# Where the first expert's weights may land: a new memory layout, earlier first loads, and 4 MB gate-and-up loads in a two-block transformer kernel

## The chip, the cores and the metric

One core of a Trainium2 chip runs the whole program. The metric is device time in microseconds (us); three runs before the change gave 1537.29, 1537.30 and 1537.64 us, median 1537.3.

## The reference, cut to what matters

Two transformer blocks on 256 tokens of width 1024, all in float32. The change touches the end of the second block: cross attention to 256 memory rows (4 heads of 128), then a mixture of 16 experts in which every expert takes its 32 best tokens, then a last norm.

```python
x = first_block(...)                                   # mixer + SwiGLU
x = x + concat(pool, mlstm, attention) @ w_out         # second block
# cross attention; mem @ ca_wkv gives k, v; 4 heads of 128
q = rmsnorm(x, norm_mem_g) @ ca_wq                     # 1024 -> 512
x = x + (softmax(q k^T * 128**-0.5) v) @ ca_wo         # 512 -> 1024
# experts
h = rmsnorm(x, norm_ffn_g)
aff = softmax(h @ router_w)                            # 256 x 16
gates, idx = top_k(aff.T, 32)                          # 32 tokens per expert
for e in range(16):
    ga, up = split(h[idx[e]] @ w_gu[e])                # w_gu[e]: 1024 x 4096, 16.8 MB
    y[e] = (silu(ga) * up) @ w_down[e]                 # w_down[e]: 2048 x 1024, 8.4 MB
x = x + scatter_add(y * gates)
return rmsnorm(x, final_norm_g)
```

The experts' weights are 402.7 MB, each byte used once.

## The kernel before, in words

All loads are issued by SyncE (SP), which takes its instructions in order: a load that waits holds up every load behind it. A layer under the kernel (tile pools) records which memory each tile occupies and makes an instruction wait for the last reader or writer of whatever lay there before. The order of instructions on each engine comes from that layer's planner, which mixes independent work; a load that names `queued(e_last)` keeps its place behind the one before it. Loads share eight completion semaphores in rotation, so each also waits until the load eight before it has landed.

`cross` (line 988) loads `ca_wq` in two 1 MB units and splits each into a high and a low part for three-pass products; then for each half t of the tokens come q, the scores against `mK`, a softmax, the values with `mV` into the tile `o`, and the product of `o` with `ca_wo` (line 1035), whose result goes to x. `route` (1040) transposes x and computes the router's logits.

`moe` (1061) loads the first expert's weights before the routing is known: `eload` issues 2 MB loads (128 partitions of 16 KB) into 12 slots. Eight slots are pools `e0` to `e7` on the right side of the memory, four are buffers of the pool `big`, which held the split weights. An expert needs eight gate-and-up loads (block k holds input features 128k to 128k+127, line 1151) and four down loads, so the first expert fills the 12 slots once, and the 13th load waits until TensorE has read the first slot. The products read each slot with eight matmuls (line 1154), or eight for a down load (1187).

The top-k chain (1093 to 1120) and the gather `xs` (1136) come before the first expert product. The last expert's down weights come in column pieces (line 1234: seven loads of 1 MB, then 0.5, 0.25 and 0.25 MB), so that the last piece leaves little work behind it.

`xt` is the pool of the normalised, transposed input (tiles `xh`, `xl`); `mkv` holds `mK` and `mV`; `rawp` holds the loads before they are split; `ca` holds `o`.

## Time and profile before

| | |
|---|---|
| median of three runs | 1537.3 us |
| profiled execution: time, span of its core | 1536.87 us, 1535.2 us |
| TensorE busy, share of the span | 1190.9 us, 78% |
| VectorE, ScalarE busy | 434.3 us, 28%; 351.7 us, 23% |
| DMA queue of SP: bytes, share of 16 engines' span | 501.86 MB, 82.0% |
| chain that ended last, share by engine | DMA 54%, PE 2%, SP's queue 2% |

The span is the time from the first to the last instruction; 1.7 us lie around it. The chain of waits is followed back from the last instruction to whatever released each step. In a timeline a row gives start, length and instructions merged (x). "SPq" is SP's queue; a load is "landed" when its semaphore has been raised.

### The profile page before, as it was taken

Reading aid. Unit: us, or ns where it says so; the run is one execution under the profiler, and the core shown is the slowest. Engines: PE = TensorE matmul, PEld = TensorE weight load, DVE = VectorE, ACT = ScalarE, POOL = GpSimd, SP = SyncE. Lnnn points to the kernel's source line nnn. Section 1 sums busy time; section 2 is a strip of 40 time slices with the busy share of each in tenths; the row PEclk is TensorE's granted clock in tenths of the full one; section 3 lists DMA queues with packets and bytes.
Section 4 is the critical chain, followed back from the end, with each engine's and each line's share of the span. In section 5 each row is a group of like instructions: output and inputs, shape, how many; then the busy total and the mean of one; then the engine's idle time right before and its main releaser. Section 6 shows DMA issues by size and latency. Waiting matters only on the chain.

```text
span 1535.2 us, 17874 instructions
## 1 busy us (share of the span) xinstructions
PE 1190.9 (78%) x7685; PEld 677.8 (44%) x7685; DVE 434.3 (28%) x851; ACT 351.7 (23%) x608; POOL 5.0 (0%) x16
## 2 busy tenths in 40 slices
PE   7999998999999999696765656666656666566665
PEld 5988988999978776221121111112111112111112
DVE  6744667544577764300000000000000000000002
ACT  6554545443456733000000000000000000000002
POOL 1000000000000000000000000000000000000000
PEclk9999999999999999797888878879788689888798
DMA  9754547555533369899999999999999999999996
GB/s 301 222 165 140 163 138 230 190 182 188 182 108 115 111 234 429 370 427 428 426 428 429 425 428 427 427 427 426 428 428 426 428 426 428 427 427 427 427 424 243
DMA packets 109103, 503.00 MB, mean 328 GB/s; under 512 B 10059, under 2 KB 64095, under 8 KB 84960
## 3 DMA queue, kind: packets, MB, share of 16 engines
q1 hardware_dynamic: 109024, 501.86, 82.0%
q8 instruction: 60, 0.98, 0.3%
q14 instruction: 19, 0.16, 0.0%
HBM read 500.79 MB, written 1.05 MB: 327 GB/s over the span
## 4 chain that ended last, share of the span: by engine, by line
DMA 54%; PE 2%; SPq 2%; DVE 1%; issue 0%; ACT 0%; DVEq 0%
DMA eraw<-in_expert_w_gu_dram 36%; DMA eraw<-in_expert_w_down_dram 18%; SPq L1234 2%; PE sm L1154 1%; PE sm L1187 1%; PE sm L1136 0%; DVE tk L1109 0%; DVE m L1108 0%; PE acc L1201 0%; DVE OH L1120 0%; DVE x L1243 0%; ACT L1174 0%; PE sm L1178 0%; DVE es L1175 0%; DVE eraw L1251 0%
## 5 line engine op out<-in xcount | busy, mean ns | idle before, releaser
L1154 PE MATMUL sm<-eraw,xs 128*32 128x512 f32 x2048 | 324.3, 742 | 190.2 <-DMA eraw<-in_expert_w_gu_dram 190.2
L1154 PEld LDWEIGHTS sm<-eraw,xs 128*32 128x32 f32 x2048 | 62.5, 123 | 425.6 <-DMA eraw<-in_expert_w_gu_dram 290.7
L1187 PE MATMUL sm<-eraw,aT 128*32 128x512 f32 (+2 forms) x1088 | 170.3, 762 | 86.8 <-DMA eraw<-in_expert_w_down_dram 79.4
L68 DVE TENSOR_TENSOR whl<-raw,whl 128x1024 fp32r<-128x1024 f32 x166 | 198.8, 1221 | 116.9 <-ACT whl L67 116.7
L67 ACT ACTIVATE whl<-raw 128x1024 fp32r<-128x1024 f32 x166 | 168.3, 1052 | 86.0 <-issue 56.1
L1175 DVE SCALAR_TENSOR_TENSOR es<-sm,rsl,es 128x512 f32<-128x512 f32 x16 | 12.0, 751 | 463.0 <-PE sm L1154 460.0
L1187 PEld LDWEIGHTS sm<-eraw,aT 128*32 128x32 f32 x1088 | 34.7, 128 | 202.9 <-DMA eraw<-in_expert_w_down_dram 125.0
L1174 ACT ACTIVATE es<-sm,rsl 128x512 f32<-128x512 f32 x16 | 11.0, 687 | 426.1 <-PE sm L1154 426.1
L86 PE MATMUL acc<-xh,whl 128*128 128x256 f32 x704 | 94.2, 283 | 0.0
L86 PE MATMUL sm<-xh,whl 128*128 128x256 f32 x704 | 92.3, 284 | 0.8 <-ACT xh L118 0.8
L86 PEld LDWEIGHTS sm<-xh,whl 128*128 128x128 f32 x704 | 88.7, 192 | 1.8 <-ACT xh L118 1.2
L86 PEld LDWEIGHTS acc<-xh,whl 128*128 128x128 f32 x704 | 87.4, 188 | 0.8
L1199 DVE COPY ys<-sm 128x512 f32<-128x512 f32 (+2 forms) x18 | 11.4, 632 | 242.1 <-PE acc L1201 237.6
L86 PE MATMUL acc<-whl,xh 128*128 128x512 f32 x256 | 70.5, 407 | 0.7 <-DVE rstd L127 0.5
L1201 PE MATMUL acc<-ys,ogT 128*128 128x512 f32 (+2 forms) x136 | 67.0, 617 | 5.1 <-DVE ys L1199 4.3
L1197 ACT ACTIVATE ys<-sm 128x512 f32<-128x512 f32 x16 | 9.6, 597 | 232.9 <-PE sm L1187 232.9
L86 PE MATMUL acc<-whl,aH 128*128 128x512 f32 x176 | 55.9, 390 | 0.0
L86 PEld LDWEIGHTS acc<-whl,xh 128*128 128x128 f32 x256 | 47.3, 190 | 13.7 <-ACT xh L118 1.4
L86 PE MATMUL acc<-xl,whl 128*128 128x256 f32 x352 | 50.9, 283 | 0.0
L86 PE MATMUL sm<-xl,whl 128*128 128x256 f32 x352 | 49.0, 281 | 0.0
L1201 PEld LDWEIGHTS acc<-ys,ogT 128*128 128x128 f32 x136 | 24.2, 202 | 54.1 <-issue 20.5
L86 PEld LDWEIGHTS acc<-xl,whl 128*128 128x128 f32 x352 | 45.3, 189 | 0.4
(361 smaller groups left out, 1099.8 us busy)
## 6 DMA issues: line engine op xcount, KB each, us to landing
eraw<-in_expert_w_gu_dram SPq DMA_DIRECT2D x128, 2048.0 KB, 39.1
eraw<-in_expert_w_down_dram SPq DMA_DIRECT2D x60, 2048.0 KB, 39.1
raw<-in_w_in_dram SPq DMA_DIRECT2D x34, 1024.0 KB, 5.5
raw<-in_w_gate_dram SPq DMA_DIRECT2D x11, 1024.0 KB, 5.3
raw<-in_w_up_dram SPq DMA_DIRECT2D x11, 1024.0 KB, 5.5
raw<-in_w_down_dram SPq DMA_DIRECT2D x11, 1024.0 KB, 4.9
raw<-in_w_out_dram SPq DMA_DIRECT2D x8, 1024.0 KB, 5.7
eraw<-in_expert_w_down_dram SPq DMA_DIRECT2D x7, 1024.0 KB, 27.8
```

Source lines behind the costliest of these rows:

```text
L67: nc.scalar.activation(H[:, k], raw[:, k], AF.Copy)
L68: self.at["L"] = nc.vector.tensor_tensor(L[:, k], raw[:, k], H[:, k].bitcast(F32), OP.subtract).ins
L86: nc.tensor.matmul(out, l[i], r[j], start=first and p == 0 and q == 0, stop=last and p == 2 and q == n - 1)
L1154: nc.tensor.matmul(dst[32 * j:32 * j + 32, :], xs[:, k, 32 * q:32 * q + 32], raw[:, o + 512 * j:o + 512 * j + 512], start=k == 0, stop=k = ...
L1174: nc.scalar.activation(s, G, AF.Silu, scale=rs)
L1175: nc.vector.scalar_tensor_tensor(s, U, rs, s, OP.mult, OP.mult)
L1187: nc.tensor.matmul(y[c0][32 * c:32 * c + 32, 0:n], aT[:, c, 32 * j:32 * j + 32], raw[:, o:o + n], start=j == 0, stop=j == 3, tile_position ...
L1197: nc.scalar.activation(ys, y[c0][:, 0:n], AF.Copy)
L1199: nc.vector.tensor_copy(ys, y[c0][:, 0:n])
L1201: nc.tensor.matmul(out[t], ogT[:, t * 128:(t + 1) * 128], ys, start=first, stop=last)
L1234: nc.sync.dma_start(raws[j].rearrange("p (i n) -> p i n", i=4)[:, :, c0:c0 + m], rows(j)[:, :, c0:c0 + m])
```

## The change

1. Feature order. Block k of the expert input is no longer features 128k to 128k+127 but every second feature of a group of 256 (`feats`). The transposes of x in `route` and in the gather, the router's weights and the gain `gT` follow this order, so that the rows of two blocks lie side by side in memory: a partition's part of blocks k and k+1 is 32 KB in one piece.
2. Memory. `mkv` moves to the left side, under `big`, and takes `o`; the pairs of high and low parts become one tile of 16 KB (`xhl`, `memHL`).
3. First expert. Four slots (`r0` to `r3`) are opened in `cross`. Its first four loads are chained in SP's order with `ca_wo`: two behind `ca_wq`, then the first half of `ca_wo`, two more, then the second half. The next eight take slots `l0` to `l3`, `xt` and `l4` to `l6`; `l0` to `l6` are opened when `rawp`, `big` and `mkv` are closed. The product with `ca_wo` runs column half by column half.
4. From the third expert on. The slots are opened anew as six of 32 KB. Gate-and-up weights come in four 4 MB loads per expert; down weights still in 2 MB loads, two to a slot.
5. The last expert. The first two of four down blocks come whole (2 MB each); the other two in column pieces as before.

SP's queue at the end of cross attention. `raw` are the loads of `ca_wq` and `ca_wo`, `eraw` the expert loads, `gain` the gain before cross attention; behind "waits" stand the semaphores (DMAHW: landed loads; PE, DVE, Activation: work done by that engine). Before:

```order
L50 DMA raw<-in_ca_wq_dram 128x4x512 [waits DMAHW6_49,DVE_49,Activation_49]
L50 DMA raw<-in_ca_wq_dram 128x4x512 [waits DMAHW7_49,DVE_49,Activation_49]
L50 DMA raw<-in_ca_wo_dram 128x4x512 [waits DMAHW0_49,DVE_49]
L50 DMA raw<-in_ca_wo_dram 128x4x512 [waits DMAHW1_49,DVE_49]
L1084 DMA eraw<-in_expert_w_gu_dram 128x4096 [waits PE_49,Pool_49]
L1084 DMA eraw<-in_expert_w_gu_dram 128x4096 [waits PE_49]
L1084 DMA eraw<-in_expert_w_gu_dram 128x4096 x3
L1084 DMA eraw<-in_expert_w_gu_dram 128x4096 [waits DMAHW2_49,DVE_49,PE_49]
L1084 DMA eraw<-in_expert_w_gu_dram 128x4096 [waits DMAHW3_49]
L1084 DMA eraw<-in_expert_w_gu_dram 128x4096 [waits DMAHW4_49]
L1084 DMA eraw<-in_expert_w_down_dram 128x4096 [waits DMAHW5_49,PE_49]
```

Now:

```order
L56 DMA raw<-in_ca_wq_dram 128x4x512 [waits DMAHW5_49,DVE_49,Activation_49]
L149 DMA gain<-in_norm_mem_g_dram 128x1024
L56 DMA raw<-in_ca_wq_dram 128x4x512 [waits DMAHW6_49,DVE_49,Activation_49]
L1069 DMA eraw<-in_expert_w_gu_dram 128x4096 [waits PE_49,Pool_49]
L1069 DMA eraw<-in_expert_w_gu_dram 128x4096 [waits DVE_49,PE_49]
L56 DMA raw<-in_ca_wo_dram 128x4x512 [waits DMAHW7_49,DVE_49]
L1069 DMA eraw<-in_expert_w_gu_dram 128x4096 [waits PE_49]
L1069 DMA eraw<-in_expert_w_gu_dram 128x4096
L56 DMA raw<-in_ca_wo_dram 128x4x512 [waits DMAHW0_49,DVE_49]
L1069 DMA eraw<-in_expert_w_gu_dram 128x4096 [waits DMAHW1_49,PE_49,Activation_49]
L1069 DMA eraw<-in_expert_w_gu_dram 128x4096 [waits DMAHW2_49]
L1069 DMA eraw<-in_expert_w_gu_dram 128x4096 [waits DMAHW3_49,DVE_49]
```

Four expert loads moved ahead of the last `ca_wo` load, and the fifth now waits for TensorE and ScalarE. Its slot, `l0`, lies from byte 31552 to 47936 of each partition; `o` lies from 28480 to 32576, so the two share the last 1024 bytes of `o`. The semaphore value that the load waits for is reached by the last matmul of `o` with `ca_wo` for the second half of the tokens (L1056); ScalarE's is the write of `o`.

TensorE at the same place: `mV` the values, `raw,o` the product with `ca_wo`, `ident,x` the transposes of x, `rw,xf` the router's logits. Before:

```order
L1023 MATMUL po<-apT,mV 128x128 x4
L1035 MATMUL acc<-raw,o 128x512 x3
L982 MATMUL sm<-ident,aE 128x128 x4
L1048 MATMUL at<-ident,x 128x128 x8
L1023 MATMUL po<-apT,mV 128x128 x4
L1059 MATMUL at<-rw,xf 128x16 x4
L1035 MATMUL acc<-raw,o 128x512
L1059 MATMUL at<-rw,xf 128x16 x4
L1035 MATMUL acc<-raw,o 128x512 x7
L1048 MATMUL at<-ident,x 128x128 x8
```

Now:

```order
L1045 MATMUL po<-apT,mV 128x128 x4
L1090 MATMUL at<-ident,x 128x128 x4
L991 MATMUL sm<-ident,aE 128x128 x4
L1045 MATMUL po<-apT,mV 128x128 x4
L1056 MATMUL acc<-raw,o 128x512 x5
L1090 MATMUL at<-ident,x 128x128 x4
L1101 MATMUL at<-rw,xf 128x16 x4
L1056 MATMUL acc<-raw,o 128x512
L1101 MATMUL at<-rw,xf 128x16 x4
L1056 MATMUL acc<-raw,o 128x512 x6
L1090 MATMUL at<-ident,x 128x128 x8
```

Behind the last matmuls on the values (`mV`) there were 8 of the 16 products with `ca_wo`; now there are 12, with four more transposes among them.

The diff (left out: the renamed arguments of `mem_T`, which now uses `pair_T`, and the closing of a pool at the end):

```diff
@@ -18,6 +18,12 @@
 EPS = 1e-6
 NEG = -1e30
 D = 1024
+def feats(k):
+    o = 256 * (k // 2) + k % 2
+    return slice(o, o + 255, 2)
 def bcast(ap1d, parts=128):
@@ -154,12 +160,16 @@
             return ss[:, 2:3]
         return ss[:, 0:1]
+    def pair_T(self, pool, name, **kw):
+        HL = self.sb(pool, [128, 2, 8, 256], name, F32R, **kw)
+        return HL[:, 0], HL[:, 1]
     def norm_T(self, x, gname):
         nc = self.nc
         g = self.gain(gname)
-        H = self.sb(self.xt, [128, 8, 256], "xh", F32R, tag="xh")
-        L = self.sb(self.xt, [128, 8, 256], "xl", F32R, tag="xl")
+        H, L = self.pair_T(self.xt, "xhl", tag="e")
         def factor(t):
             h = self.work.tile([128, D], F32, name="hn", tag="work")
@@ -221,7 +231,9 @@
         self.xt = self.open("xt", 1, self.xtp, "right")
         self.NR, self.NH = 3, 4
         self.ep = self.open("ep", 1)
-        self.big = self.open("big", 1)
+        bigst = ExitStack()
+        self.mkv = self.open("mkv", 1, bigst)
+        self.big = self.open("big", 1, bigst)
         rawst = ExitStack()
         self.rawp = self.open("rawp", 1, rawst)
         st = ExitStack()
@@ -235,8 +247,6 @@
         nc.sync.dma_start(x[:, 1, :], xr[:, 1, :])
         first = [self.unit(a["w_in"][0], u, 1024) for u in range(2)]
         self.constants()
-        mkv = ExitStack()
-        self.mkv = self.open("mkv", 1, mkv, "right")
         memp = ExitStack()
         self.memp = self.open("memp", 1, memp, "right")
         for t in range(2):
@@ -245,7 +255,7 @@
         xT = self.block1_ffn(xT, wg)
         xT = self.block2_mix(*xT, memp, st)
         self.cross(xT)
-        self.close(rawst, mkv, self.xtp)
+        self.close(rawst, bigst)
         self.moe()
         self.psum_st.close()
...
@@ -504,10 +514,9 @@
         nc.tensor.matmul(po[:, 128:256], va[:, 1, h * 128:(h + 1) * 128], pT[:, 256:384], start=False, stop=True)
         nc.scalar.activation(qT[:, h, :], po[:, 0:256], AF.Copy)
-    def mem_T(self, pool, tags=(None, None), psum="sm"):
+    def mem_T(self, pool, psum="sm"):
         nc, tc = self.nc, self.tc
-        H = self.sb(pool, [128, 8, 256], "memH", F32R, tag=tags[0])
-        L = self.sb(pool, [128, 8, 256], "memL", F32R, tag=tags[1])
+        H, L = self.pair_T(pool, "memHL", tag="e")
         m = self.rawp.tile([128, 2, D], F32, name="mem", tag="raw", bufs=self.NR)
         nc.sync.dma_start(m, self.a["mem_2"][0].rearrange("(t p) d -> p t d", p=128))
         for t in range(2):
...
@@ -990,16 +999,29 @@
         NE = 16
         with ExitStack() as es:
             ca, cw = self.open("ca", 1, es), self.open("caw", 2, es)
-            o = self.sb(ca, [128, 4, 256], "o")
+            o = self.sb(self.mkv, [128, 4, 256], "o")
+            self.early = ExitStack()
+            self.ewt = [self.open("r%d" % i, 1, self.early, "right") for i in range(4)]
+            self.e_last, self.loaded = [], []
             rt = self.ep
             rw = self.sb(rt, [128, 8, NE], "rw")
-            nc.sync.dma_start(rw, a["router_w_2"][0].rearrange("(k p) e -> p k e", p=128))
+            nc.sync.dma_start(rw.rearrange("p (k i) e -> p k i e", i=2),
+                              a["router_w_2"][0].rearrange("(k p i) e -> p k i e", p=128, i=2))
             gT = self.gT = self.sb(rt, [128, 8], "gT")
-            nc.sync.dma_start(gT, a["norm_ffn_g_2"][0].rearrange("(k p) -> p k", p=128))
+            nc.sync.dma_start(gT.rearrange("p (k i) -> p k i", i=2),
+                              a["norm_ffn_g_2"][0].rearrange("(k p i) -> p k i", p=128, i=2))
             nc.vector.tensor_tensor(rw, rw, gT[:, :, None].to_broadcast([128, 8, NE]), OP.mult)
             self.rw = rw
             w = self.cols(a["ca_wq_2"][0], 0)
+            for k in range(2):
+                self.loaded.append(self.gu_block(self.ewt[k], k))
+            wo = [self.chained(lambda: self.unit(a["ca_wo_2"][0], 0, 0))]
+            for k in range(2, 4):
+                self.loaded.append(self.gu_block(self.ewt[k], k))
+            wo.append(self.chained(lambda: self.unit(a["ca_wo_2"][0], 0, 512)))
             for t in range(2):
                 c = slice(t * 128, (t + 1) * 128)
                 acc = self.gemm_t(xT, w, t)
@@ -1027,14 +1049,35 @@
             self.r4, self.r4_ins, self.logits = [None] * 2, [None] * 2, [None] * 2
             self.rc = self.sb(rt, [128, 2], "rc")
-            w = [self.unit(a["ca_wo_2"][0], 0, 512 * c) for c in range(2)]
             for t in range(2):
                 acc = [self.ps("acc") for _ in range(2)]
-                for k in range(4):
-                    for c in range(2):
-                        nc.tensor.matmul(acc[c], o[:, k, t * 128:(t + 1) * 128], w[c][:, k, :], start=k == 0, stop=k == 3)
+                for c in range(2):
+                    for k in range(4):
+                        nc.tensor.matmul(acc[c], o[:, k, t * 128:(t + 1) * 128], wo[c][:, k, :], start=k == 0, stop=k == 3)
                 self.add_x(t, acc)
                 self.route(t, cw)
+    def chained(self, f):
+        n = len(self.nc.cur_bb.bb.instructions)
+        with self.queued(self.e_last):
+            r = f()
+        return r
+    def eload(self, dst, src):
+        with self.queued(self.e_last):
+            self.e_last[:] = [self.nc.sync.dma_start(dst, src).ins]
+    def gu_block(self, pool, k, e=0):
+        raw = pool.tile([128, 4096], F32, name="eraw", tag="e")
+        self.eload(raw, self.gu_rows(e, k)[:, k % 2])
+        return raw
+    def gu_rows(self, e, k):
+        o = 256 * (k // 2)
+        return self.a["expert_w_gu_2"][0][e, o:o + 256, :].rearrange("(p i) n -> p i n", i=2)
     def route(self, t, cw):
@@ -1044,8 +1087,7 @@
         for q in range(2):
             p = self.ps("at")
             for k in range(4):
-                c = 4 * q + k
-                nc.tensor.transpose(p[:, k * 128:(k + 1) * 128], x[:, t, c * 128:(c + 1) * 128], self.ident)
+                nc.tensor.transpose(p[:, k * 128:(k + 1) * 128], x[:, t, feats(4 * q + k)], self.ident)
             p = p.rearrange("p (k c) -> p k c", k=4)
             if q == 0:
                 nc.vector.tensor_copy(xf[:, 0:4], p)
@@ -1061,29 +1103,25 @@
     def moe(self):
         tc, nc, a = self.tc, self.nc, self.a
         NE, CAP = 16, 32
-        wgu, wdn = a["expert_w_gu_2"][0], a["expert_w_down_2"][0]
+        wdn = a["expert_w_down_2"][0]
         with ExitStack() as es:
             ep, x = self.ep, self.x
             ew = self.open("ew", 1, es)
             OH = self.sb(ep, [128, 2, NE, CAP], "OH")
             aff = self.sb(ep, [128, 2, NE], "aff")
-            e_ = [(self.open("e%d" % i, 1, es, "right"), "e", 1) for i in range(8)]
-            hl = (self.big, "hl", self.NH)
-            slots = e_[2:5] + [hl] * 2 + e_[:1] + [hl] * 2 + e_[1:2] + e_[5:8]
-            n_unit, e_last = [0], []
+            slot_st = ExitStack()
+            left = [self.open("l%d" % i, 1, slot_st) for i in range(7)]
+            pools = self.ewt + left[0:4] + [self.xt] + left[4:7]
+            n_slot = [4]
             def slot():
-                pool, tag, bufs = slots[n_unit[0] % len(slots)]
-                n_unit[0] += 1
-                return pool.tile([128, 4096], F32, name="eraw", tag=tag, bufs=bufs)
-            def eload(src):
-                raw = slot()
-                with self.queued(e_last):
-                    e_last[:] = [nc.sync.dma_start(raw, src).ins]
-                return raw
+                pool = pools[n_slot[0] % len(pools)]
+                n_slot[0] += 1
+                return pool.tile([128, 4096 if len(pools) == 12 else 8192], F32, name="eraw", tag="e")
+            eload = self.eload
             io = self.sb(ep, [128, CAP], "io")
             nc.gpsimd.iota(io, pattern=[[1, CAP]], base=1, channel_multiplier=0, allow_small_or_imprecise_dtypes=True)
             st = self.small.tile([128, 16], F32, name="rs", tag="st8", bufs=4)
@@ -1133,7 +1171,7 @@
                             if i == 0:
                                 pg[kk] = self.ps()
                             for t in range(2):
-                                nc.tensor.matmul(pg[kk][:, i * 128:(i + 1) * 128], x[:, t, k * 128:(k + 1) * 128],
+                                nc.tensor.matmul(pg[kk][:, i * 128:(i + 1) * 128], x[:, t, feats(k)],
                                                  OH[:, t, e:e + 4, :].rearrange("p e s -> p (e s)"), start=t == 0, stop=t == 1)
                         kk, i = divmod(k0, 4)
                         nc.vector.tensor_tensor(xs[:, k0:k0 + n, :],
@@ -1147,8 +1185,22 @@
                         gather(0, 1)
                         gather(1, 1)
                 G, U = self.ps(), self.ps()
+                if e == 2:
+                    self.close(slot_st, self.early, self.xtp)
+                    left = [self.open("ll%d" % i, 1, slot_st) for i in range(6)]
+                    pools, n_slot[0] = [left[i] for i in (4, 5, 0, 1, 2, 3)], 0
                 for k in range(8):
-                    raw = eload(wgu[e, 128 * k:128 * k + 128, :])
+                    src = self.gu_rows(e, k)
+                    if e == 0 and k < 4:
+                        raw = self.loaded[k]
+                    elif e < 2:
+                        raw = slot()
+                        eload(raw, src[:, k % 2])
+                    else:
+                        if k % 2 == 0:
+                            both = slot()
+                            eload(both, src.rearrange("p i n -> p (i n)"))
+                        raw = both[:, 4096 * (k % 2):4096 * (k % 2) + 4096]
                     for o, dst in ((0, G), (2048, U)):
                         for j in range(4):
                             nc.tensor.matmul(dst[32 * j:32 * j + 32, :], xs[:, k, 32 * q:32 * q + 32],
@@ -1202,7 +1254,13 @@
                 if e < NE - 1:
                     for j in range(4):
-                        raw = eload(rows(j).rearrange("p i n -> p (i n)"))
+                        if e < 2:
+                            raw = slot()
+                        else:
+                            if j % 2 == 0:
+                                both = slot()
+                            raw = both[:, 4096 * (j % 2):4096 * (j % 2) + 4096]
+                        eload(raw, rows(j).rearrange("p i n -> p (i n)"))
                         for n in range(2):
                             down(j, raw, 512 * n, 512)
                     for n in range(2):
@@ -1219,7 +1277,7 @@
                 p = self.ps()
                 nc.tensor.matmul(p, self.ones[0:1, :], grow[:, 512 * n:512 * n + 512], start=True, stop=True)
                 nc.scalar.activation(g[:, 512 * n:512 * n + 512], p, AF.Copy)
-            fo = slot()[:, 0:2 * D].rearrange("p (t n) -> p t n", t=2)
+            fo = end[:, 4 * D:6 * D].rearrange("p (t n) -> p t n", t=2)
             ss = self.small.tile([128, 16], F32, name="ss", tag="st1", bufs=4)
             sq = ss[:, 0:8].rearrange("p (t n) -> p t n", t=2)
             raws, y[768], y[896] = {}, self.ps(), self.ps()
@@ -1228,7 +1286,16 @@
                 c = slice(c0, c0 + n)
                 for j in range(4):
                     if i == 0:
-                        raws[j] = slot()
+                        if j % 2 == 0:
+                            both = slot()
+                        raws[j] = both[:, 4096 * (j % 2):4096 * (j % 2) + 4096]
+                    if j < 2:
+                        if i == 0:
+                            nc.sync.dma_start(raws[j], rows(j).rearrange("p i n -> p (i n)"))
+                            for o, w in cuts:
+                                down(j, raws[j], o, w)
+                        continue
                     m = 512 if j < 3 else n
                     if c0 < 768 or j == 3:
                         nc.sync.dma_start(raws[j].rearrange("p (i n) -> p i n", i=4)[:, :, c0:c0 + m],
...
```

## Rows read from the trace of the kernel before

**Rows 1.** The page: DMA share and GB/s in 40 slices of 38.4 us.
```profile
DMA  9754547555533369899999999999999999999996
GB/s 301 222 165 140 163 138 230 190 182 188 182 108 115 111 234 429 370 427 428 426 428 429 425 428 427 427 427 426 428 428 426 428 426 428 427 427 427 427 424 243
```
**Rows 2.** Chain of waits in order of time: start us, length us, what.
```profile
692.22 39.23 DMA eraw<-in_expert_w_gu_dram
...
1510.40 11.34 DMA eraw<-in_expert_w_down_dram
...
1521.79 0.43 PE sm L1187 x8
```
**Rows 3.** Windows: stretch, length, busy us by engine (instructions), PEclk, DMA share, GB/s.
```profile
570.10:614.60 44.50, 43.10 (x209) 29.30 (x208) 22.64 (x68) 16.63 (x46) 0.18 (x1) 1.00 0.98 411
614.60:627.50 12.90, 5.03 (x24) 2.73 (x27) 8.58 (x32) 0.45 (x2) 0.18 (x1) 0.53 0.91 373
627.50:630.30 2.80, 2.80 (x20) 0.78 (x16) 0.29 (x1) 0.00 (x0) 0.00 (x0) 0.71 0.00 0
700.00:1470.00 770.00, 496.38 (x2991) 123.67 (x2994) 32.84 (x62) 29.45 (x52) 0.00 (x0) 0.82 1.01 427
1500.00:1510.00 10.00, 8.49 (x48) 2.60 (x48) 0.75 (x1) 2.48 (x4) 0.00 (x0) 0.83 1.05 387
```
**Rows 4.** SP's timeline; 570.12 and 588.04 are parts of the x8 row.
```profile
544.81 2.65 SPq L50 DMA_DIRECT2D raw<-in_ca_wq_dram  x2
...
561.00 28.32 SPq L1084 DMA_DIRECT2D eraw<-in_expert_w_gu_dram  x8
...
570.12 2.15 SPq L1084 DMA_DIRECT2D eraw<-in_expert_w_gu_dram  x4
...
588.04 1.28 SPq L1084 DMA_DIRECT2D eraw<-in_expert_w_gu_dram  x3
...
602.59 12.85 SPq L1084 DMA_DIRECT2D eraw<-in_expert_w_down_dram  x4
629.37 2.81 SPq L1084 DMA_DIRECT2D eraw<-in_expert_w_gu_dram  x2
```
**Rows 5.** SP's waits, 545 to 632 us: total us, times, longest us.
```profile
SPq L1084 <- PE sm L1154: 15.9, 2, 13.8
...
SPq L1084 <- PE sm L86: 8.7, 1, 8.7
```
**Rows 6.** TensorE's timeline, end of cross attention (a matmul on f32 is two records).
```profile
587.85 1.02 PE L1035 MATMUL acc<-raw,o 128*128 128x512 f32 x2
...
601.40 1.16 PE L1023 MATMUL po<-apT,mV 128*128 128x128 f32 x8
602.40 0.96 PE L1059 MATMUL at<-rw,xf 128*128 128x16 f32 x8
...
604.96 6.25 PE L1035 MATMUL acc<-raw,o 128*128 128x512 f32 x14
611.14 0.66 PE L1048 MATMUL at<-ident,x 128*128 128x128 f32 x4
```
**Rows 7.** The page: DMA issues, KB each, median us from issue to landing.
```profile
eraw<-in_expert_w_gu_dram SPq DMA_DIRECT2D x128, 2048.0 KB, 39.1
...
raw<-in_w_up_dram SPq DMA_DIRECT2D x11, 1024.0 KB, 5.5
```
**Rows 8.** TensorE's timeline: first expert, mid-stream, the last gate-and-up load.
```profile
629.87 1.92 PE L1154 MATMUL sm<-eraw,xs 128*32 128x512 f32 x16
...
632.36 1.92 PE L1154 MATMUL sm<-eraw,xs 128*32 128x512 f32 x16
...
716.80 3.64 PE L1154 MATMUL sm<-eraw,xs 128*32 128x512 f32 x16 [1.26 <-DMA eraw<-in_expert_w_gu_dram]
...
1500.58 1.92 PE L1154 MATMUL sm<-eraw,xs 128*32 128x512 f32 x16 [1.70 <-DMA eraw<-in_expert_w_gu_dram]
```
**Rows 9.** VectorE's timeline: the scaling that needs the gain before cross attention.
```profile
567.20 1.42 DVE L172 SCALAR_TENSOR_TENSOR hn<-x,rstd,gain 128x512 f32<-128x512 f32 x2
```

More of the change, by code (lines that the diff above doesn't have):

```diff
@@ L396, in block1_mix @@
                     self.attn1_head(mw, h, qT, kT, va, cc, crow[:, h % 2, :])
-            self.mem_T(self.memp, ("memH", "memL"))
+            self.mem_T(self.memp)
             mH = self.sb(m1, [128, 8, 256], "mH", F32R, tag="B")
@@ L706, in block2_mix @@
             self.attn2(mw, qT, kT, av, yH, yL)
-            self.mem_T(self.xt, ("xh", "xl"), "acc")
+            self.mem_T(self.xt, "acc")
             self.mem_V(0)
@@ L1253, in moe @@
                 nc.sync.dma_start(self.out[t * 128:(t + 1) * 128, :], fo[:, t, :])
+            self.close(slot_st)
 def consts():
```

## The prediction

> **What bounds the kernel now.** I read the slices of the page first [rows 1]: up to slice 14 the DMA engines are mostly at half load and TensorE is full; from slice 15 (576 us) to the last one DMA moves some 427 GB/s, slice 16 (614 to 653 us) apart, with 370. Then the chain of waits [rows 2]: from 692 us on it is one expert load after another, and the pieces of 39.1 us are eight 2 MB loads each, since a load waits for the one eight before it. That is 39.1 / 8 = 4.9 us a load, and the window from 700 to 1470 us shows the same 427 GB/s at a DMA share of 1.01, with TensorE busy 64% of it [rows 3]. So the expert part is a stream: its end is the time at which it starts to run without a gap, plus 4.9 us for each load still to come. After its last byte (1521.7 us) come 13.5 us of products and norm [rows 2], which the change leaves alone.
>
> The question is thus where the stream starts and how many loads are behind it by then. SP issues the first expert load at 561.0 us, four more at 570, three at 588, two at 602.6 and two at 614.6; the 13th, at 629.4 us, waits 13.8 us for TensorE to read the first slot [rows 4, 5]. In between DMA is hardly ever idle: 411 GB/s from 570 to 614.6 us, then 373, and only 2.8 us at zero, from 627.5 to 630.3 [rows 3]. So at 629.4 us twelve loads are in memory and 180 are to come (192 of 2 MB in all), and from there to the last byte the stream takes 892.4 us, with every loss in it.
>
> **The change part by part.**
>
> *Earlier loads.* The first load now stands right behind `ca_wq` and can go at about 547.5 us, 13.5 us sooner. The second waits for the same last products of `w_out` as before (the 8.7 us wait of rows 5, over at 570); the first half of `ca_wo` is behind it in SP's order, then loads three and four and the other half. That is 8.4 MB, at 411 GB/s over by about 591 us. `ca_wo` is not late by that: its first half lands at about 578 (3.15 MB from 570), its second at 591. The first product with it began at 587.9 us before [rows 6], and the second half is read only behind the last products on the values, which stood at 601.4.
>
> *The fifth load.* This is the place that decides. It waits until the last product of `o` with `ca_wo` is done, because its slot shares 1024 bytes with `o`; the seven others of the first expert stand behind it on SP, although their slots are free. Before, that product ended at 611.2 us [rows 6], while loads six to ten went [rows 4] at 588 and 602.6. So from 591 us until the fifth load DMA has nothing to move, in a stretch that it filled at 411 GB/s.
>
> When is the product over now? TensorE is full there (43.1 of 44.5 us [rows 3]) and has the same work, so not before 611.2 - 1.4 = 609.8 us. In the new order 12 products, four transposes and eight logit products stand behind the last products on the values: 12 x 0.89 (6.25 us for 14 records, seven matmuls) + 0.66 + 1.9 = 13.3 us [rows 6]. If the values came as late as before, at 602.4, that would be 615.7 us; with four products fewer ahead of them (3.6 us) they come sooner, as far as the softmax chain allows. I take 613, between the two.
>
> *What it costs.* At that time four loads are in memory and 188 to come; at 629.4 us before, twelve and 180. Both streams start on idle engines. The end moves by (613 - 629.4) + 8 x 4.9 = -16.4 + 39.2 = +22.8 us. The earlier start of the first four loads buys nothing by itself: what used to hold the stream was full slots at 629.4 us, and twelve loads were in by then.
>
> *The first expert's products.* They took a load every 2.5 us, the second from 629.9 us [rows 8], and so the fifth from 637, some 2 us later now through the routing chain behind the product; loads five to eight land from 619 to 634 us. Not late. The 13th load then waits for TensorE as before, but with loads still queued, so DMA does not notice.
>
> *4 MB loads.* Rows of 2 KB run at 387 GB/s, rows of 16 KB at 427 [rows 3]. A packet of 2 KB then takes an engine 2048 x 16 / 387 = 84.7 ns, one of 16 KB 613.9 ns, so 36.9 ns a KB (of 1000 bytes) and 9.1 ns fixed. A 32 KB packet in place of two saves 9.1 ns, eight times a load: 0.07 us, for 56 loads (14 experts, 4 each) -4.1 us. No run shows a packet of 32 KB. Bounds: 0, if it is cut in two again, and -8.1 us, if it carries no fixed cost at all; I take the middle, which the two rows give.
>
> *32 KB slots.* A slot is free when both halves have been read. A load's eight matmuls take 1.9 to 3.6 us [rows 8], so a slot is read some 7 us after it landed, the first down slot later by the silu chain; meanwhile the five other slots, 5 x 9.7 = 48 us, are queued. No gap: 0 us. The same holds where the slots are opened anew (third expert): the second 4 MB load waits for the second expert's first down product, with 14.7 us of down loads and 9.7 us of the first 4 MB load still queued.
>
> *The last expert.* 4 MB move from 2 KB to 16 KB rows: 4.19 MB / 0.387 - 4.19 / 0.427 = 10.8 - 9.8 = -1.0 us. The last 4 MB gate-and-up load gives TensorE two blocks to read at once after it lands, 2 to 4 us more [rows 8], under some 21 us of down loads behind it; cover is left, at worst 3 us late.
>
> *Nothing:* the feature order (the transposes and gathers are as many as before), the pairs in one tile, and the gain's load between the two of `ca_wq` (0.5 MB, needed at 567.2 us [rows 9]).
>
> Sum: +22.8 - 4.1 - 1.0 = +17.7 us on the profiled 1536.9 us, 1554.6; the median of the runs is 0.4 us above the profiled one: 1555 us, 1.2% slower.
>
> **The rivals.**
>
> *The loads go out under cross attention after all (faster).* If the fifth load's wait were over early, the stream would lose nothing at the head. The point from which it decides: with T for the fifth load's issue the change is T - 629.4 + 39.2 - 5.1, which is zero at T = 595.3 us. Sooner still, and the 13th load binds as before: no more than -5.1 us, 1532 us. For it: the eight loads were issued from 570 to 615 us before, and seven of the eight slots are free. Against it: the queue of SP in the new order, with `o` read to the last product at 610 us or later.
>
> *Half the loads, half the fixed times (faster).* If each load carried a fixed time of its own, 56 fewer would save it. A load of 1 MB alone takes 5.5 us to land [rows 7], of which 2.5 us are bytes at 427 GB/s: 3.0 us fixed, 168 us in all, 1387 us. Against it: in the queue a 2 MB load takes 4.9 us in all, and 2.10 MB at 36.9 ns a KB on 16 engines are 4.84 us, so what a queued load carries is under 0.1 us; the fixed time lies beside seven other loads. The Trainium skill, "DMA: Bandwidth & Descriptors", section "Anatomy of one DMA", gives 2.0 us fixed plus bytes at 436 GB/s; by it the 56 loads would save an estimated 112 us and the time be 1443 us. The rows speak against reading it so: a 2 MB load would take 6.8 us by it, and 4.9 are measured with others behind it.
>
> *Coarse slots leave a gap per expert (slower).* If the refill of a slot came after the queue had run dry, each of 14 experts would lose, say, one 2 MB load's time, 4.9 us: 69 us, 1624 us. Against it: the 48 us queued.
>
> *The wait is longer.* `ca_wo` late, or a stalled softmax chain: 620 us for T gives 1562 us.
>
> **How the numbers follow.** The forecast, fifth load at 609.8 to 616 us and packets 0 to -8.1 us: 0.86. With the ends of both, 1555 - 3.2 - 4.0 = 1548 to 1555 + 3 + 4.1 = 1562. A longer wait, 0.04; a gap per expert, 0.02; loads under cross attention, 0.05; fixed times, 0.01; and 0.02 for a sum near zero. Range 1547 to 1562. Two runs of this kernel can be told apart by some 0.2% (3 us): faster 0.06, same 0.02, slower 0.92.
>
> **What would show it.** In the profile after: SP issues the first expert load at about 547, three at 570 to 571, the fifth at about 613, with some 40 us waited for the product with `ca_wo`; in the window from 592 to 612 us DMA moves next to nothing; slice 15 falls from 429 to some 200 GB/s, slice 16 rises to over 400. From then on 427 to 431 GB/s without a gap. The products of the first expert begin 1 to 4 us later. The last byte lands at about 1539 us, and 13.5 us follow. I am wrong if the fifth load goes before 595 us, if the stream runs at another rate than 427 to 434 GB/s, or if it stops between experts.

## The result: 1557.5 us, 1.3% slower

The changed kernel takes 1557.54 us (median of four runs, 1556.74 to 1559.85); the ratio to the kernel before is 1.0133, interval 1.0118 to 1.0149. The forecast was 1555 us and slower. The profiled execution took 1559.85 us, the slowest of the four, with a span of 1558.1; the span before was 1535.2. So there are 22.9 us to explain, and the last byte alone lands 19.6 us later.

The page's slices, DMA share and GB/s, of the kernel after (the same view as [rows 1]):

```profile
DMA  9655447565533263999999999999999999999995
GB/s 300 215 163 157 142 151 228 185 191 181 184 110 113 92 261 138 427 426 430 430 430 430 430 429 432 430 428 432 430 426 433 429 427 431 429 429 431 429 430 220
```

A slice is now 39.0 us. Slice 15 (584 to 623 us) fell from 429 to 138 GB/s: that is the loss. Slice 14 rose from 234 to 261, the early loads. From slice 16 to slice 38 there are 426 to 433 GB/s, where before, from slice 17 on, there were 424 to 429.

SyncE's timeline after (start, length, instructions merged), which answers to [rows 4]:

```profile
540.85 0.37 SPq L56 DMA_DIRECT2D raw<-in_w_out_dram  x1
...
547.65 22.68 SPq L1069 DMA_DIRECT2D eraw<-in_expert_w_gu_dram  x2
570.77 0.38 SPq L56 DMA_DIRECT2D raw<-in_ca_wo_dram  x1
571.21 1.31 SPq L1069 DMA_DIRECT2D eraw<-in_expert_w_gu_dram  x2
572.62 0.43 SPq L56 DMA_DIRECT2D raw<-in_ca_wo_dram  x1
616.46 1.85 SPq L1069 DMA_DIRECT2D eraw<-in_expert_w_gu_dram  x4
618.40 2.24 SPq L1069 DMA_DIRECT2D eraw<-in_expert_w_down_dram  x4
634.47 25.21 SPq L1069 DMA_DIRECT2D eraw<-in_expert_w_gu_dram  x8
```

Four expert loads and both halves of `ca_wo` are issued by 573 us; then SyncE issues nothing for 43 us, and at 616.46 the fifth load and seven more go out within 4 us. The 13th goes at 634.47, 5.1 us later than before. SyncE's longest wait after, 540 to 640 us (total, times, longest), the view of [rows 5], names who was waited for:

```profile
SPq L1069 <- PE acc L1056: 43.3, 1, 43.3
```

L1056 is the product of `o` with `ca_wo`. Windows after (stretch, length, busy us by engine, granted TensorE clock, DMA share, GB/s), the view of [rows 3]:

```profile
571.00:592.00 21.00, 19.34 (x100) 14.86 (x99) 10.37 (x28) 8.49 (x22) 0.00 (x0) 1.00 0.99 395
592.00:612.00 20.00, 17.45 (x74) 10.31 (x73) 7.64 (x25) 6.19 (x19) 0.18 (x1) 0.91 0.01 3
700.00:1470.00 770.00, 488.48 (x2990) 136.78 (x2982) 31.00 (x59) 29.84 (x53) 0.00 (x0) 0.80 1.00 430
1525.00:1535.00 10.00, 9.06 (x48) 2.89 (x44) 0.75 (x1) 2.48 (x4) 0.00 (x0) 0.67 1.02 387
1541.20:1541.70 0.50, 0.50 (x3) 0.26 (x2) 0.00 (x0) 0.00 (x0) 0.00 (x0) 1.00 0.30 78
1541.70:1550.00 8.30, 5.47 (x63) 3.07 (x61) 5.44 (x14) 4.07 (x16) 0.00 (x0) 1.00 0.00 0
```

From 592 to 612 us DMA moves 3 GB/s, where it had moved some 411 [rows 3]. The stream itself is a little faster, 430 GB/s for 427. The last two rows bracket the last byte, at 1541.7. The row from 1525 to 1535 us shows a granted clock of 0.67, so part of that stretch ran at 1.2 GHz and part at 2.4, the two levels, while TensorE is nearly full; that counts below.

Before, the last byte was at 1522.1, where DMA falls to zero in the same view. The prediction took 1521.7, the end of the last load in the chain [rows 2], and so 13.5 us behind it; by these rows it is 13.1:

```profile
1521.60:1522.10 0.50, 0.31 (x8) 0.16 (x8) 0.40 (x1) 0.00 (x0) 0.00 (x0) 1.00 0.16 40
1522.10:1530.00 7.90, 2.99 (x25) 1.88 (x20) 4.87 (x23) 3.23 (x13) 0.00 (x0) 0.80 0.00 0
```

TensorE at the end of cross attention, after (the stretch of [rows 6]):

```profile
599.41 0.63 PE L991 MATMUL sm<-ident,aE 128*128 128x128 f32 x4 [1.59 <-DVE aE L987]
600.78 1.28 PE L1045 MATMUL po<-apT,mV 128*128 128x128 f32 x8 [0.75 <-ACT apT L994]
601.85 6.07 PE L1056 MATMUL acc<-raw,o 128*128 128x512 f32 x10
607.85 0.74 PE L1090 MATMUL at<-ident,x 128*128 128x128 f32 x4
609.24 1.10 PE L1056 MATMUL acc<-raw,o 128*128 128x512 f32 x2
610.99 5.40 PE L1056 MATMUL acc<-raw,o 128*128 128x512 f32 x12
```

The last products on the values (L1045) end at 602.1 us, as late as before (602.6), although four products fewer stand ahead of them: TensorE now waits 1.59 and 0.75 us for the softmax there. VectorE's last scaling of the softmax weights (`aE`) stands where it stood; its row before, then after:

```profile
598.89 0.62 DVE L978 TENSOR_SCALAR aE<-aE,st 128x256 f32<-128x256 f32 x2
```
```profile
598.90 0.62 DVE L987 TENSOR_SCALAR aE<-aE,st 128x256 f32<-128x256 f32 x2
```

Before, TensorE filled the time until then with those four products. The last product with `ca_wo` ends at 616.4, and the fifth load goes 0.1 us later.

The chain of waits after (start, length, what), the view of [rows 2]:

```profile
602.06 5.87 PE acc L1056 x10
...
1532.15 7.73 PE sm L1239 x80
```

The product with `ca_wo` now stands in it, and it ends in TensorE's work and no longer in a load, as it did with the 11.34 us of the last down load: at the last byte TensorE is behind.

The page's DMA issues after (KB each, median us to landing), for [rows 7]: of 128 gate-and-up loads of 2 MB 16 are left, the others have become 56 of 4 MB.

```profile
eraw<-in_expert_w_gu_dram SPq DMA_DIRECT2D x56, 4096.0 KB, 53.2
eraw<-in_expert_w_gu_dram SPq DMA_DIRECT2D x16, 2048.0 KB, 26.5
```

### The profile page after: what moved, and what is told of

It reads as the page before. It is cut to its first block, busy times and chain, and to the rows that moved or that the text cites. A ratio compares the mean times of both kernels' runs of the same rounds, so it can differ in the third digit from the quotient of the medians.

```text
span 1558.1 us, 17731 instructions
## 1 busy us (share of the span) xinstructions
PE 1192.9 (77%) x7685; PEld 694.5 (45%) x7685; DVE 434.0 (28%) x851; ACT 352.3 (23%) x608; POOL 4.9 (0%) x16
## 4 chain that ended last, share of the span: by engine, by line
PE 57%; DMA 21%; another core or an unknown queue 11%; DVE 6%; ACT 2%; issue 1%; SPq 0%; DVEq 0%; ACTq 0%
PE acc L92 18%; DMA eraw<-in_expert_w_down_dram 15%; PE sm L1206 13%; PE sm L92 9%; PE sm L1239 7%; DMA eraw<-in_expert_w_gu_dram 5%; PE acc L1253 3%; PE sm L1174 1%; PE acc L1056 1%; DVE whl L74 1%; DVE rstd L138 1%; DVE es L1227 0%; PE sm L1230 0%; DVE ys L1251 0%
## 5 line engine op out<-in xcount | busy, mean ns | idle before, releaser
L1206 PE MATMUL sm<-eraw,xs 128*32 128x512 f32 x2048 | 333.5, 808 | 220.4 <-DMA eraw<-in_expert_w_gu_dram 220.4
L1206 PEld LDWEIGHTS sm<-eraw,xs 128*32 128x32 f32 x2048 | 78.2, 142 | 456.8 <-issue 228.4
L1239 PE MATMUL sm<-eraw,aT 128*32 128x512 f32 (+2 forms) x1088 | 158.3, 723 | 63.8 <-DMA eraw<-in_expert_w_down_dram 53.2
L92 PE MATMUL acc<-xhl,whl 128*128 128x256 f32 x1056 | 132.2, 283 | 0.0
L92 PE MATMUL sm<-xhl,whl 128*128 128x256 f32 x1056 | 128.4, 283 | 0.9 <-ACT xhl L124 0.9
L92 PEld LDWEIGHTS sm<-xhl,whl 128*128 128x128 f32 x1056 | 128.0, 191 | 1.9 <-ACT xhl L124 1.3
L92 PEld LDWEIGHTS acc<-xhl,whl 128*128 128x128 f32 x1056 | 127.2, 189 | 1.1
L92 PE MATMUL acc<-whl,xhl 128*128 128x512 f32 x384 | 96.1, 403 | 0.7 <-DVE rstd L133 0.5
L92 PEld LDWEIGHTS acc<-whl,xhl 128*128 128x128 f32 x384 | 71.1, 190 | 19.6 <-DVE whl L74 1.8
L1253 PE MATMUL acc<-ys,ogT 128*128 128x512 f32 (+2 forms) x136 | 65.3, 604 | 15.4 <-DVE ys L1251 14.4
L1253 PEld LDWEIGHTS acc<-ys,ogT 128*128 128x128 f32 x136 | 23.3, 194 | 64.0 <-DVE ys L1251 27.7
L92 PEld LDWEIGHTS acc<-whl,aH 128*128 128x128 f32 x176 | 33.0, 188 | 6.7
```

Of the source, the lines that this page charges most:

```text
L92: nc.tensor.matmul(out, l[i], r[j], start=first and p == 0 and q == 0, stop=last and p == 2 and q == n - 1)
L1206: nc.tensor.matmul(dst[32 * j:32 * j + 32, :], xs[:, k, 32 * q:32 * q + 32], raw[:, o + 512 * j:o + 512 * j + 512], start=k == 0, stop=k = ...
L1239: nc.tensor.matmul(y[c0][32 * c:32 * c + 32, 0:n], aT[:, c, 32 * j:32 * j + 32], raw[:, o:o + n], start=j == 0, stop=j == 3, tile_position ...
L1253: nc.tensor.matmul(out[t], ogT[:, t * 128:(t + 1) * 128], ys, start=first, stop=last)
```

## The experiments

Theory: the whole loss is the fifth load's wait for `o`; the early loads buy nothing; the 4 MB loads gain 9 ns a packet. Rivals: the 4 MB loads or the 32 KB slots lose time; the early start matters; the longer tail comes from the last 4 MB load. "Tail" is the time from the last byte to the end of the span: 13.1 us before, 16.4 in the changed kernel's first profile. The runs e0_after, e1_pad, e2_halves and e3_last were on one chip, the other four below on another; the kernel before took 1537.71 us on the first and 1537.72 on the second, so times from the two are compared directly.

**The changed kernel again (e0_after).**

> The changed kernel once more, on the same chip as the three beside it, as the base for differences of 2 to 4 us: 1555 to 1560 us. It tells no theory apart by itself. In its profile the fifth load should again stand at about 616 us, the 13th at about 634, and some 16 us should lie between the last byte and the end.

Measured: 1557.15 us (1556.04 to 1558.19), ratio 1.0126 (1.0112 to 1.0140). The fifth load went at 615.86 us, the last byte landed at 1541.2, the span ended at 1555.4. So the last byte is where it was, and the tail is 14.2 us in place of 16.4, where the expectation had some 16: the tail of one and the same kernel varies by 2.2 us. TensorE's timeline of this execution, then of the first one, at the last gate-and-up load and the last down loads:

```profile
1520.86 6.16 PE L1206 MATMUL sm<-eraw,xs 128*32 128x512 f32 x32 [4.38 <-DMA eraw<-in_expert_w_gu_dram]
...
1530.55 4.52 PE L1239 MATMUL sm<-eraw,aT 128*32 128x512 f32 x72
1536.01 1.06 PE L1239 MATMUL sm<-eraw,aT 128*32 128x512 f32 x8 [0.95 <-DMA eraw<-in_expert_w_down_dram]
1537.86 1.98 PE L1253 MATMUL acc<-ys,ogT 128*128 128x512 f32 x4 [0.78 <-ACT ys L1249]
```
```profile
1521.32 6.28 PE L1206 MATMUL sm<-eraw,xs 128*32 128x512 f32 x32 [6.08 <-DMA eraw<-in_expert_w_gu_dram]
...
1532.08 7.75 PE L1239 MATMUL sm<-eraw,aT 128*32 128x512 f32 x80
1540.62 1.98 PE L1253 MATMUL acc<-ys,ogT 128*128 128x512 f32 x4 [0.79 <-ACT ys L1249]
```

The same products on the down weights took 4.52 + 1.06 us with an idle 0.95 between them here, and 7.75 us without any in the first: there the clock was low (0.67 from 1525 to 1535 us, here 0.95, the row below), and the scatter product behind them (L1253) began 2.8 us later.

```profile
1525.00:1535.00 10.00, 9.06 (x96) 3.62 (x88) 0.75 (x1) 2.48 (x4) 0.00 (x0) 0.95 1.00 378
```

**One KB between `o` and l0 (e1_pad).**

```diff
+            self.sb(self.open("pad", 1, slot_st), [128, 256], "pad")
             left = [self.open("l%d" % i, 1, slot_st) for i in range(7)]
```

> One tile of 1 KB more is opened in front of slot l0, so that l0 no longer shares bytes with o; nothing else is moved. Theory A (the whole loss is the fifth load's wait for the last product with ca_wo): loads five and six wait only for old loads to land and go at about 573 us, seven and eight at about 587; the tenth still waits for the last product with ca_wo, at 616, but with four loads queued or under way until then, so DMA runs from 571 to about 630. The 13th load stays at about 634.5, since the routing chain behind the product is as late as in the changed kernel. From there 180 loads at 4.92 us (925.2 us from 616.5 to the last byte, over 188 loads) end at 1520, and with 16.4 us of tail and 1.7 around the span the time is 1538 us (1535 to 1541), 20 us under the changed kernel. Rival B (the 4 MB loads or the 32 KB slots cost it, the wait is covered): it stays at 1554 to 1558. Rival C (the early loads starve ca_wo, and this holds the rest): the fifth load goes early and the time falls by less than 10 us.

Measured: 1536.19 us, ratio to before 0.9994 (0.9985 to 1.0003): 21 us faster than the changed kernel, level with before. SyncE's timeline and a window of this kernel:

```profile
574.17 16.02 SPq L1069 DMA_DIRECT2D eraw<-in_expert_w_gu_dram  x4
590.28 29.80 SPq L1069 DMA_DIRECT2D eraw<-in_expert_w_down_dram  x4
633.98 17.21 SPq L1069 DMA_DIRECT2D eraw<-in_expert_w_gu_dram  x8
```
```profile
592.00:612.00 20.00, 17.45 (x81) 10.96 (x80) 7.65 (x25) 6.67 (x20) 0.18 (x1) 1.00 1.02 431
```

The fifth load goes at 574 us, and DMA runs through the stretch at 431 GB/s in place of 3. The 13th still goes at 634.0, as late as in the changed kernel. From it to the last byte (1520.2) are 886.2 us; it was 892.7 before. Theory A holds; B and C fall. The tile also moves `l0` to `l6` by 1 KB; the next experiment leaves them where they are.

**The slot that touches `o` last (e7_slotlast).**

```diff
-            pools = self.ewt + left[0:4] + [self.xt] + left[4:7]
+            pools = self.ewt + left[1:4] + [self.xt] + left[4:7] + left[0:1]
```

> One line: of the eight slots opened last, l0, the one that shares bytes with o, is taken last in place of first, by the 12th load. Nothing is laid out anew, no byte is added. Theory A (it is the order in which the slots are taken that puts the wait at the fifth load, and not the layout): the fifth load at about 573, the 10th waits for the last product with ca_wo (through the slot that held ca_wo) at 616 as with the tile, the 13th at about 634: 1536 us (1534 to 1539), as with the tile. Rival B (the tile's gain came from what it moved elsewhere): 1545 us or more.

Measured: 1538.51 us (1535.52 to 1539.74), ratio 1.0004 (0.9995 to 1.0012): 18.6 us under the changed kernel by an order of slots alone: theory A holds, B falls, and the loss is not the layout's. It is some 2 us above the kernel with the tile: the ninth load, the first down load, waits for the last product here until 615.56 us (the second row below), because it takes `l4`, the slot that the tenth load takes with the tile, and DMA runs dry for 2.7 us until then. SyncE's timeline, then a window:

```profile
573.99 16.61 SPq L1069 DMA_DIRECT2D eraw<-in_expert_w_gu_dram  x4
615.56 4.67 SPq L1069 DMA_DIRECT2D eraw<-in_expert_w_down_dram  x4
```
```profile
613.80:616.50 2.70, 2.38 (x10) 1.24 (x9) 0.94 (x2) 0.15 (x1) 0.00 (x0) 1.00 0.00 0
```

The expectation had named the tenth load for this wait; eight loads and not nine were out by 616 us.

**No early loads, the overlap kept (e6_late).**

```diff
-            for k in range(2):
-                self.loaded.append(self.gu_block(self.ewt[k], k))
             wo = [self.chained(lambda: self.unit(a["ca_wo_2"][0], 0, 0))]
-            for k in range(2, 4):
-                self.loaded.append(self.gu_block(self.ewt[k], k))
             wo.append(self.chained(lambda: self.unit(a["ca_wo_2"][0], 0, 512)))
+            for k in range(4):
+                self.loaded.append(self.gu_block(self.ewt[k], k))
```

> Both halves of ca_wo ahead of all expert loads, but without the tile: l0 still shares 1024 bytes with o. Theory A (the end is the fifth load's issue plus 188 loads, whatever the four loads ahead of it do): the first load goes 14 us later than in the changed kernel, at about 561, and the fifth 5 us sooner, at about 611, since four products fewer stand behind the values; so the time falls by 5 us, to 1552 (1549 to 1555). Rival B (the early start counts): the time rises by up to 14 us, to 1571. Rival C (the last product does not come sooner): 1557, no change.

Measured: 1552.32 us (1552.07 to 1553.03), 4.8 us under the changed kernel (1557.15 in e0_after). SyncE's timeline (the row at 610.80 is a part of the x8 row) and its longest wait:

```profile
540.84 0.37 SPq L56 DMA_DIRECT2D raw<-in_w_out_dram  x1
...
561.42 51.23 SPq L1067 DMA_DIRECT2D eraw<-in_expert_w_gu_dram  x8
...
610.80 1.85 SPq L1067 DMA_DIRECT2D eraw<-in_expert_w_gu_dram  x4
```
```profile
SPq L1067 <- PE acc L1054: 39.5, 1, 39.5
```

The first load goes 14 us later than in the changed kernel, the fifth at 610.80 in place of 615.86, 5.1 us sooner, and the time follows the fifth. So the time goes with T, as the prediction's formula has it, and the early loads are worth less than nothing: with them the planner puts 12 products behind the values, without them 7 (14 records; the expectations had counted 8). The window from 592 to 612 us has TensorE busy 19.56 us here and 17.45 in the changed kernel.

Not all of the 5.1 us is the order. From the last load of `w_out`, which stands ahead of every load that the edit moves, to the fifth load, it takes 70.0 us here and 75.6 in both executions of the changed kernel. In e2_halves and e3_last, which have the changed kernel's order up to here, it takes 73.9. TensorE's granted clock from 592 to 612 us was 0.91 in the two executions of the changed kernel and 1.00 in the other three. So the order costs 3.9 us, and the lower clock 1.7; what comes ahead of the `w_out` load differs by up to 2.3 us between executions.

**The tile, and no early loads (e5_pad_late):** both edits above together.

> The 1 KB tile in front of l0, and in SP's order both halves of ca_wo stand ahead of all expert loads, so that the first expert load is no longer the early one; feature order, slots and 4 MB loads stay. Behind the last products on the values TensorE then has 8 of the 16 products with ca_wo again, as before the change, in place of 12. Theory A (the early loads buy nothing and cost some 5 us, since through the planner they push four products, and with them the routing chain, behind the values): the first load at about 561, the 13th at about 629.4 in place of 634.0 with the tile alone; 886 us from there to the last byte, as with the tile alone, then 14 us of tail: 1532 us (1529 to 1535), 4 us under the tile alone and 5 under the kernel before. Rival B (the early loads are worth the 14 us that they go sooner): 1540 us and more. Rival C (the 13th load is late for another reason in the new layout): 1536, as with the tile alone.

Measured: 1531.23 us (1530.89 to 1535.04), ratio to before 0.9964 (0.9952 to 0.9977): the fastest of all, 0.36% under the kernel before. SyncE's timeline:

```profile
561.54 27.55 SPq L1067 DMA_DIRECT2D eraw<-in_expert_w_gu_dram  x8
...
628.93 17.17 SPq L1067 DMA_DIRECT2D eraw<-in_expert_w_gu_dram  x8
```

The 13th load goes at 628.93, 5.05 us sooner than with the tile alone, and the time is 4.96 us less. Counted from the last load of `w_out` (540.97 us here, 541.93 with the tile alone), the 13th goes 4.1 us sooner, which agrees with the 3.9 above. From it to the last byte (1515.2) are 886.3 us again. What is left of the change, the 4 MB loads and the last expert, is thus a gain: 6.4 us in the stream, against 892.7 before.

**4 MB loads cut in two (e2_halves).**

```diff
                         if k % 2 == 0:
                             both = slot()
-                            eload(both, src.rearrange("p i n -> p (i n)"))
+                            if not (e < NE - 1):
+                                eload(both, src.rearrange("p i n -> p (i n)"))
                         raw = both[:, 4096 * (k % 2):4096 * (k % 2) + 4096]
+                        if e < NE - 1:
+                            eload(raw, src[:, k % 2])
```

> Every gate-and-up load of experts 2 to 14 is issued as two of 2 MB (packets of 16 KB) into the same 32 KB slots; the last expert keeps its 4 MB loads, and the head is untouched. Theory A (a packet has 9 ns of its own, whatever its size): 52 loads x 8 x 9.1 ns = 3.8 us slower than the changed kernel, 1561 us, and 427 GB/s in place of 430 in the stream. Rival B (a 32 KB packet costs as much as two of 16 KB, and the stream's 430 GB/s come from elsewhere): no difference, within 1 us. Rival C (each load has a fixed time of some 2 to 3 us): 52 loads more cost 104 to 156 us, over 1660 us. Rival D (4 MB loads keep TensorE waiting and so the slots full): faster than the changed kernel.

Measured: 1561.86 us (1560.49 to 1562.76), 4.7 us over the changed kernel of the same test. From the fifth load (616.50) to the last byte (1545.8) it takes 929.3 us, the changed kernel 925.3 (615.86 to 1541.2): 4.0 us for 52 loads, where 3.8 were expected. The two profiled executions differ by 5.7 us in all; the rest is the fifth load (0.6 later) and the tail (1.0 longer). In the changed kernel's trace a 16 KB packet of the stream takes 613 ns in the median and one of 32 KB 1215, 11 ns less than two of 16 KB. Windows of this kernel (the end of cross attention, then the stream), and two rows of SyncE's timeline:

```profile
592.00:612.00 20.00, 17.45 (x86) 11.24 (x85) 7.65 (x25) 6.53 (x20) 0.18 (x1) 1.00 0.09 33
700.00:1470.00 770.00, 500.11 (x2994) 125.19 (x2986) 30.50 (x58) 30.20 (x53) 0.00 (x0) 0.81 1.01 428
```
```profile
542.59 0.37 SPq L56 DMA_DIRECT2D raw<-in_w_out_dram  x1
...
616.50 1.85 SPq L1069 DMA_DIRECT2D eraw<-in_expert_w_gu_dram  x4
```

428 GB/s, and 430 with 4 MB loads. A has it; B's "no difference" is excluded by the stream's length, C by its size, D by its sign.

**The last expert's 4 MB loads cut in two (e3_last):** the same edit with `e == NE - 1`.

> Only the last expert's gate-and-up weights come in 2 MB loads instead of 4 MB; all else is the changed kernel. Theory A (the time after the last byte grew from 13.1 to 16.4 us because the last 4 MB load hands TensorE two blocks at once, and TensorE then works to the end without a wait): 3 us less behind the last byte, 0.3 us more for packets, so 2.7 us faster than the changed kernel, 1555 us, and some 13.5 us between last byte and end. Rival B (the tail grew by the last down blocks, whole instead of in column pieces): no difference, 16 us of tail remain.

Measured: 1557.80 us (1557.50 to 1559.18), no faster. Theory A, mine, falls; B's "no difference" fits, and b2 below tests it. The last byte lands at 1541.8 and 15.7 us of tail remain, in TensorE's timeline of this kernel:

```profile
1536.71 1.06 PE L1242 MATMUL sm<-eraw,aT 128*32 128x512 f32 x8 [1.58 <-DMA eraw<-in_expert_w_down_dram]
1538.55 3.44 PE L1256 MATMUL acc<-ys,ogT 128*128 128x512 f32 x4 [0.78 <-ACT ys L1252]
1541.92 1.91 PE L1242 MATMUL sm<-eraw,aT 128*32 128x256 f32 x40
```

TensorE had caught up with the loads by 1536.7 us, so the two blocks at once did no harm. What is late stands behind that: the 40 matmuls on the last column pieces begin only after the scatter product (L1256), 3.44 us here at a low clock and 1.98 in the repeated run above.

**The last expert as before (b2):** the fastest kernel, and in the last expert

```diff
-                    if j < 2:
+                    if j < 0:
```

> The kernel with the tile and ca_wo ahead, and the last expert's down weights in column pieces as before the change (all four blocks). Theory A (with two blocks whole, TensorE is behind at the last byte, 14.2 us of tail in place of 13.1, against 1.0 us less for their bytes): the tail shrinks by 1 us, the bytes take 1 us more, and the time is that of the same kernel with two blocks whole within 1 us, 1532 us. Rival B (the longer tail is due to TensorE's lower granted clock, 0.67 in the last stretch of the changed kernel): the tail is as long as with the blocks whole and the time 1 us more. Rival C (the pieces are worth 3 us): 1529.

Measured: 1532.12 us (1531.54 to 1534.07), ratio 0.9967 (0.9954 to 0.9979). From the 13th load (629.40) to the last byte (1516.8) are 887.4 us, 1.1 more than with two blocks whole; the tail is 13.6 us in place of 14.3. So the whole blocks give 1.1 us of bytes and take some 0.7 of tail back. C falls. The time, 0.9 us more, fits A and B alike; the tail speaks for A, since with the blocks whole it was 14.2 or 14.3 us in five profiled executions (e0_after, e1_pad, e5_pad_late, e6_late, e7_slotlast). It was longer, 16.4, 15.2 and 15.7 us, only in the three (the changed kernel's first, e2_halves, e3_last) in which the last products on the down weights or the scatter product ran at a low clock. So the whole blocks account for 0.7 us of tail (1.1 against the kernel before), and the clock, as B has it, for another 2.2 in the changed kernel's first profile. Part 5 of the change is worth next to nothing.

## Why the prediction was right, and where its sizes were off

*What bounds the kernel* held: every kernel here ends at (issue of the load that starts the unbroken stream) + (loads left) x 4.9 us + tail; from the traces a load takes 4.92 to 4.96 us.

*The fifth load* was the right place and the right wait, 43.3 us for the product with `ca_wo`. Its time was off: T was taken at 613 us, between 609.8 and 615.7, and was 616.46, just past the upper bound. I had let the values come sooner for the four products fewer ahead of them, up to 3.6 us; they came 0.5 us sooner, because the softmax chain ended when it had ended before (598.89 and 598.90 us, the rows above), and TensorE waits the 1.59 and 0.75 us for it. That by itself puts T near 615, inside the bounds. The bound was passed because five of the products ran at a lower clock: 6.07 us for ten records, 4.46 in the kernel with the tile; the window shows 0.91 granted after TensorE had waited. The kernel with the tile had the same two waits and was granted 1.00 there, so the waits alone do not bring the lower clock, and no run shows what does. The head's term is so (616.46 - 629.37) + 8 x 4.9 = +26.3 us, in place of +22.8.

*Earlier loads buy nothing*: right, and too mild. Through the planner's order they cost some 4 us at the full clock (3.9 by e6_late, 4.1 by e5_pad_late, from the last load of `w_out` on; the medians differ by 4.8 and 5.0). The prediction counted that order in T, but not as a price of the early loads.

*The first expert's products* were 5.1 us late at the 13th load, not 2, and it cost nothing while loads were queued, as said.

*Packets*: right. 4.0 us measured for 52 loads; 4.1 predicted for 56. *The last expert's bytes*: -1.0 predicted, 1.1 measured. The stream from the fifth load to the last byte was 6.7 us shorter than 8 x 4.9 us and the 892.7 of before make it, where these two terms give 5.1; no run assigns the other 1.6.

*32 KB slots, feature order, pairs*: nothing, right: the stream has no gap between experts, and with the tile and `ca_wo` ahead (e5_pad_late) the 13th load goes at 628.93 us, for 629.37 before.

*The tail* was the second mis-sized term: priced at 0, "at worst 3 us late", it was +3.3 in the profiled run and +1.1 in the repeated one. The cover that I named, 21 us of down loads, did hold for the last 4 MB load; the down blocks behind it, two of them whole, and a low clock made TensorE late at the last byte instead, with 1.1 us at most and 2.2 us of the 3.3. No run sets the clock, so its part rests on comparing executions.

Sum for the profiled execution: +26.3 - 6.7 + 3.3 = +22.9 us, in place of +17.7. The median was 2.3 us under that execution, about what its long tail cost. For the execution of e0_after, which is near the median, the sum is +25.7 - 6.6 + 1.1 = +20.2 us. So 1555 met 1557.5 with three terms off by +2.9, -1.5 and +1.1 us, of which the second cancels a part of the others.

The rivals fell by the same rows: the fifth load did not go under cross attention, 56 loads fewer saved microseconds and not a hundred, and no expert left a gap. The section of the Trainium skill that the prediction cites for 2.0 us a load, "Anatomy of one DMA" in "DMA: Bandwidth & Descriptors", is on loads issued from GpSimd. The loads here are issued by SyncE, and cutting 52 of them in two cost 4.0 us in all (e2_halves).

## What to carry to other kernels

When a tile is laid where another tile still lives, look up which load of an in-order queue meets the overlap first: 1 KB of 16 stopped eight loads for 43 us, and a 1 KB tile, or taking that slot last, gave 21 or 19 us back. A transfer that starts sooner is worth nothing if the stream behind it is held by a later one; price the start of the unbroken stream, not of the first load. And an edit of load order can move the compute order through a planner: read both before counting a gain.

## What the hardware showed that was not expected

Packets of 32 KB carry the fixed cost once: 430 GB/s in the stream, 428 with the same bytes in 16 KB; a packet of 32 KB takes 1215 ns, two of 16 KB 2 x 613.

Near the end of the stream TensorE is idle for 4 to 6 us of every 9.7, and the clock that it is then granted differs between two executions of the same kernel: 0.67 in one and 0.95 in the other from 1525 to 1535 us. The products on the down weights then took 7.75 us, or 4.52 and 1.06 with a wait between, and the tail 16.4 or 14.2 us. Runs of the kernel with the tile fall into groups near 1536 and near 1539 us, at mean clocks of about 0.90 and 0.88 over the whole execution; a difference of 2 to 3 us between two kernels of this kind needs several runs.
